# A cross-entropy kernel whose first load is split into two halves of 64 partitions, issued by two engines, with a new table of load widths

## The chip, the cores and the metric

The kernel runs on 1 core of one Trainium2 chip. Time is device time in microseconds of that core; smaller is better. Timed runs of one kernel lie within 0.6 us of each other, most within 0.3. The experiments ran on four chips, each beside the kernel before, whose medians there were 85.26 to 85.42. A profiled execution has a span (first to last instruction), which is 1.8 us shorter than the same execution's time.

## The reference

```python
batch, num_classes = 256, 32000          # logits float32, labels integers
log_probs = logits - np.max(logits, axis=-1, keepdims=True)
log_probs = log_probs - np.log(np.sum(np.exp(log_probs), axis=-1, keepdims=True))
return np.array([-log_probs[i, labels[i]] for i in range(batch)])
```

The kernel leaves the maximum out. Each of the 128 partitions holds two rows one after the other, 64000 columns in all. It takes exp over them with running sums, gathers the logit of each label, and writes ln(sum x exp(-logit)).

## The kernel before

```python
CHUNKS = [
    14848, 12288, 8832, 6528, 4992, 3776, 2752,
    2368, 1856, 1344, 1344, 1152, 1024, 896,
]
...
    def load(i):
        t, base = tiles[i]
        a, b = starts[i], starts[i] + CHUNKS[i]
        nc.sync.dma_start(out=t[:, a - base:b - base], in_=flat[:, a:b])
...
        for i in range(HEAD):          # HEAD = 5: the first five loads, issued at once
            load(i)
        nc.scalar.dma_start(out=lbl[:, :], in_=...)   # labels, on ScalarE's queue
        ...                                           # index arithmetic and two gathers on GpSimd
        exps(0)
        ...                                           # exps(1), then the loads 5 to 13
        nc.scalar.activation(out=eg[:, :], in_=g[:, :], func=AF.Exp, scale=-1.0)
        for i in range(2, len(CHUNKS) - 1):
            exps(i)
```

`exps(i)` is one ScalarE exp over load `i` (two where a load crosses from one row to the next), with the sum as accumulator. A hook moves SyncE's first load ahead of the opening barrier.

The softmax here doesn't subtract the row's maximum and nothing guards it: scores larger than these inputs give would overflow.

## Time and profile before

| | before |
|---|---|
| time, median | 85.26 us (85.17 to 85.44) |
| time and span of the profiled run | 85.8 us, 84.0 us |
| first load lands (first exp starts) | 20.70 us |
| second load lands | 35.91 us |
| last exp starts, ends | 79.98, 80.93 us |

The table is read from the bottom up. The end follows the last exp; ScalarE works nearly without a gap from the landing of the second load (its waits on later loads add up to 0.4 us); the DMA queue is busy all the time up to the last load (92.2% of the span). The prediction below shows the lines.

### The profile page before, as it was taken

The numbers are of one execution on the slowest core, as the hardware profiler recorded it, in microseconds if no ns is written. First come the engines' busy times: TensorE is split into PE (matmuls) and PEld (weight loads), VectorE is DVE, ScalarE is ACT, GpSimd is POOL, SyncE is SP. The second block draws the span as 40 slices with busy tenths as digits, with TensorE's granted clock in tenths as the row PEclk, the third lists the DMA queues.
The fourth block names the chain that finished last, engine by engine and source line by source line (L and its number), as shares of the span: only waits on it lengthen the run. The fifth ranks groups of instructions, "written<-read, shape, count | busy, mean of one in ns | idle before, by whom it ended". The sixth has DMA issues, their size and how long they took to land.

```text
span 84.0 us, 126 instructions
## 1 busy us (share of the span) xinstructions
PE 1.8 (2%) x6; PEld 0.3 (0%) x6; DVE 0.8 (1%) x4; ACT 58.9 (70%) x34; POOL 3.0 (4%) x10
## 2 busy tenths in 40 slices
PE   0000000000000000000000002000000000000050
PEld 0000000000000000000000000000000000000000
DVE  0000000000000000000000200000000000000000
ACT  6000000001999998089999999999999999999960
POOL 3000000000072000000000000000000000000000
DMA  9787899998999989979989999999999999999300
GB/s 424 311 368 339 368 453 453 453 453 375 515 491 421 398 374 421 454 320 521 454 370 407 448 448 403 443 428 417 396 422 418 425 412 420 414 413 405 149 0 0
DMA packets 2226, 32.77 MB, mean 390 GB/s; under 512 B 433, under 2 KB 434, under 8 KB 1202
## 3 DMA queue, kind: packets, MB, share of 16 engines
q1 hardware_dynamic: 2018, 32.77, 92.2%
q10 hardware_dynamic: 144, 0.00, 0.1%
q0 software_dynamic: 64, 0.00, 0.1%
HBM read 32.77 MB, written 0.00 MB: 390 GB/s over the span
## 4 chain that ended last, share of the span: by engine, by line
DMA 74%; issue 13%; ACT 6%; SPq 2%; PE 1%
DMA x<-in_logits_dram 42%; DMA x_tail<-in_logits_dram 33%; ACT x_tail L112 6%; SPq L100 2%; PE lane L160 1%; ACT res L120 0%; ACT x L112 0%; ACT eg L148 0%
## 5 line engine op out<-in xcount | busy, mean ns | idle before, releaser
L112 ACT ACTIVATE x<-x 128x14848 f32<-128x14848 f32 (+5 forms) x6 | 40.7, 6790 | 21.2 <-DMA x<-in_logits_dram 21.2
L112 ACT ACTIVATE x_tail<-x_tail 128x1344 f32<-128x1344 f32 (+6 forms) x8 | 12.2, 1525 | 0.4 <-DMA x_tail<-in_logits_dram 0.4
L112 ACT ACTIVATE x_mid<-x_mid 128x3776 f32<-128x3776 f32 x1 | 3.3, 3349 | 0.0
L135 POOL DMA_INDIRECT g<-in_logits_dram,idx x2 | 2.1, 1036 | 0.6 <-issue 0.3
L91 ACT ACT_TABLE_LOAD x1 | 1.3, 1283 | 0.8 <-PEq L179 0.8
L155 PE MATMUL lane<-diag,sums 128*1 128x128 f32 x2 | 0.6, 396 | 51.0 <-DVE sums L154 51.0
L112 ACT ACTIVATION_READ_ACCUMULATOR x_tail<-x_tail 128x1 f32 x8 | 1.5, 186 | 0.0
L158 PE MATMUL lane<-diag,sums 128*1 128x128 f32 x2 | 0.6, 397 | 28.7 <-DVE sums L157 28.7
L112 ACT ACTIVATION_READ_ACCUMULATOR x<-x 128x1 f32 x6 | 1.1, 187 | 0.0
L120 ACT ACTIVATE res<-lane 1x128 f32<-1x128 f32 x2 | 0.5, 264 | 0.7 <-PE lane L160 0.7
L133 POOL TENSOR_TENSOR idx<-idx,lbl 128x2 int32<-128x2 int32 x1 | 0.2, 193 | 21.4 <-DMA lbl<-in_labels_dram 21.4
L150 DVE TENSOR_SCALAR diag<-ident,eg 128x128 f32<-128x128 f32 x2 | 0.5, 285 | 46.7 <-ACT eg L148 46.7
L160 PE MATMUL lane<-diag,s_last 128*1 128x128 f32 x2 | 0.6, 394 | 0.2 <-ACT x_tail L112 0.2
L157 DVE TENSOR_REDUCE sums<-parts 128x1 f32<-128x11 f32 x1 | 0.2, 164 | 29.1 <-ACT x_tail L112 29.1
masks.py:199 POOL TENSOR_SCALAR_AFFINE_SELECT ident<-ident 128x128 f32<-128x128 f32 x1 | 0.3, 292 | 0.1
L155 PEld LDWEIGHTS lane<-diag,sums 128*1 128x1 f32 x2 | 0.1, 80 | 51.0 <-DVE sums L154 51.0
masks.py:197 POOL MEMSET ident<- 128x128 f32 x1 | 0.2, 194 | 0.0
L154 DVE TENSOR_REDUCE sums<-parts 128x1 f32<-128x3 f32 x1 | 0.2, 156 | 3.7 <-ACT x L112 3.7
L148 ACT ACTIVATE eg<-g 128x2 f32<-128x2 f32 x1 | 0.2, 188 | 0.0
L112 ACT ACTIVATION_READ_ACCUMULATOR x_mid<-x_mid 128x1 f32 x1 | 0.2, 186 | 0.0
L158 PEld LDWEIGHTS lane<-diag,sums 128*1 128x1 f32 x2 | 0.1, 80 | 29.2 <-DVE sums L157 29.2
L131 POOL IOTA idx<- 128x2 int32 x1 | 0.1, 120 | 0.5 <-POOLq L179 0.5
(5 smaller groups left out, 0.5 us busy)
## 6 DMA issues: line engine op xcount, KB each, us to landing
x<-in_logits_dram SPq DMA_DIRECT2D x1, 7424.0 KB, 20.7
x<-in_logits_dram SPq DMA_DIRECT2D x1, 6144.0 KB, 35.1
x<-in_logits_dram SPq DMA_DIRECT2D x1, 4416.0 KB, 45.0
x<-in_logits_dram SPq DMA_DIRECT2D x1, 3264.0 KB, 51.8
x<-in_logits_dram SPq DMA_DIRECT2D x1, 2496.0 KB, 57.2
x_mid<-in_logits_dram SPq DMA_DIRECT2D x1, 1888.0 KB, 17.9
x_tail<-in_logits_dram SPq DMA_DIRECT2D x1, 1376.0 KB
x_tail<-in_logits_dram SPq DMA_DIRECT2D x2, 672.0 KB, 26.8
```

The costliest lines, as they stand in the source:

```text
L91: nc.scalar.preload_act_table_set("natural_log_exp_and_others")
L100: nc.sync.dma_start(out=t[:, a - base:b - base], in_=flat[:, a:b])
L112: nc.scalar.activation(out=t[:, a - base:b - base], in_=t[:, a - base:b - base], func=AF.Exp, accum_out=acc,)
L120: nc.scalar.activation(out=res[0:1, r:ROWS * P:ROWS], in_=lane[r][:, :], func=AF.Ln)
L133: nc.gpsimd.tensor_add(out=idx[:, :], in0=idx[:, :], in1=lbl[:, 0:2 * ROWS:2])
L135: nc.gpsimd.indirect_dma_start(out=g[:, r:r + 1], out_offset=None, in_=logits[:, :], in_offset=bass.IndirectOffsetOnAxis(ap=idx[:, r:r + 1 ...
L148: nc.scalar.activation(out=eg[:, :], in_=g[:, :], func=AF.Exp, scale=-1.0)
L150: nc.vector.tensor_scalar_mul(diag[r][:, :], ident[:, :], eg[:, r:r + 1])
L154: nc.vector.reduce_sum(out=sums[:, 0:1], in_=parts[0][:, :], axis=mybir.AxisListType.X)
L155: nc.tensor.matmul(lane[0][:, :], sums[:, 0:1], diag[0][:, :], start=True, stop=True)
L158: nc.tensor.matmul(lane[1][:, :], sums[:, 1:2], diag[1][:, :], start=True, stop=False)
L160: nc.tensor.matmul(lane[1][:, :], s_last[:, :], diag[1][:, :], start=False, stop=True)
```

## The change

The intent, as I read it, is an earlier start. SyncE and ScalarE each issue half of the first load ahead of the barrier, and a new table makes the first loads wider and the last one narrower, with one load fewer.

```diff
 CHUNKS = [
-    14848, 12288, 8832, 6528, 4992, 3776, 2752,
-    2368, 1856, 1344, 1344, 1152, 1024, 896,
+    15552, 13376, 8960, 7168, 5056, 3584,
+    2816, 2176, 1536, 1280, 1024, 768, 704,
 ]
...
-    first = next(i for i in rest if i.engine == mybir.EngineType.SP and i.opcode == "DMACopy")
...
+    for engine in (mybir.EngineType.SP, mybir.EngineType.Activation):
+        first = next(i for i in rest if i.engine == engine and i.opcode == "DMACopy")
...
-        nc.sync.dma_start(out=t[:, a - base:b - base], in_=flat[:, a:b])
+        if i == 0:
+            nc.sync.dma_start(out=t[:H, a - base:b - base], in_=flat[:H, a:b])
+            nc.scalar.dma_start(out=t[H:, a - base:b - base], in_=flat[H:, a:b])
+        else:
+            nc.sync.dma_start(out=t[:, a - base:b - base], in_=flat[:, a:b])
...
-            if seen[0] == n_of[0] and i == HEAD - 1:
+            if i == turn:
                 ...                    # sum and matmul of the first row
+            if i == turn + 1:
                 log_row(0)
```

`H` is 64. The rest of the diff renames pools and writes the same slots as a list.

More of the change, by code (lines that the diff above doesn't have):

```diff
@@ L10 @@
 P = 128
+H = P // 2
 ROWS = 2
@@ L16 @@
 CHUNKS = [
-    14848, 12288, 8832, 6528, 4992, 3776, 2752,
-    2368, 1856, 1344, 1344, 1152, 1024, 896,
-]
-HEAD = 5
+    15552, 13376, 8960, 7168, 5056, 3584,
+    2816, 2176, 1536, 1280, 1024, 768, 704,
+]
+SLOTS = [0, 1, 2, 3, 4, 1]
+TAIL = len(SLOTS)
+TAIL_SLOT = 0
 def begin_first_load_before_barrier(nc):
@@ L27, in begin_first_load_before_barrier @@
     rest = list(body.instructions)
-    first = next(i for i in rest if i.engine == mybir.EngineType.SP and i.opcode == "DMACopy")
-    rest.remove(first)
     head = list(main.instructions)
-    at = next(
-        k for k, i in enumerate(head) if i.engine == mybir.EngineType.SP and i.opcode == "Drain"
-    )
-    head.insert(at, first)
+    for engine in (mybir.EngineType.SP, mybir.EngineType.Activation):
+        first = next(i for i in rest if i.engine == engine and i.opcode == "DMACopy")
+        rest.remove(first)
+        at = next(k for k, i in enumerate(head) if i.engine == engine and i.opcode == "Drain")
+        head.insert(at, first)
     main.instructions = head
@@ L63 @@
         at += n
-    head = ctx.enter_context(tc.tile_pool(name="head", bufs=1))
+    last = len(CHUNKS) - 1
+    turn = next(i for i in range(len(CHUNKS)) if starts[i] + CHUNKS[i] >= C)
+    big = ctx.enter_context(tc.tile_pool(name="big", bufs=1))
     small = ctx.enter_context(tc.tile_pool(name="small", bufs=1))
+    psum = ctx.enter_context(tc.tile_pool(name="psum", bufs=1, space=bass.MemoryType.PSUM))
+    width = {}
+    for i, s in enumerate(SLOTS):
+        width[s] = max(width.get(s, 0), CHUNKS[i])
     tiles = []
-    for i in range(HEAD):
-        tiles.append((head.tile([P, CHUNKS[i]], F32, name=f"x{i}", tag=f"slot{i}"), starts[i]))
-    mid = head.tile([P, CHUNKS[1]], F32, name="x_mid", tag="slot1")
-    tail = head.tile([P, CHUNKS[0]], F32, name="x_tail", tag="slot0")
-    tiles.append((mid, starts[HEAD]))
-    for i in range(HEAD + 1, len(CHUNKS)):
-        tiles.append((tail, starts[HEAD + 1]))
+    for i, s in enumerate(SLOTS):
+        tiles.append((big.tile([P, width[s]], F32, name=f"x{i}", tag=f"slot{s}"), starts[i]))
+    tail = big.tile([P, width[TAIL_SLOT]], F32, name="x_tail", tag=f"slot{TAIL_SLOT}")
+    assert sum(CHUNKS[TAIL:]) <= width[TAIL_SLOT]
+    tiles += [(tail, starts[TAIL])] * (len(CHUNKS) - TAIL)
     n_of = [sum(1 for ps in pieces[:-1] for q in ps if q[2] == r) for r in range(ROWS)]
@@ L83 @@
     diag = [small.tile([P, P], F32, name=f"diag{r}") for r in range(ROWS)]
-    psum = ctx.enter_context(tc.tile_pool(name="psum", bufs=1, space=bass.MemoryType.PSUM))
     lane = [psum.tile([1, P], F32, name=f"lane{r}") for r in range(ROWS)]
@@ L106, in exps @@
         for a, b, r in pieces[i]:
-            if i == len(CHUNKS) - 1:
+            if i == last:
                 acc = s_last[:, :]
@@ L124 @@
     with tc.manual_schedule():
-        for i in range(HEAD):
+        first = len(set(SLOTS))
+        for i in range(first):
             load(i)
@@ L140 @@
             )
-        exps(0)
-        for i in range(HEAD + 1, len(CHUNKS)):
-            if i == HEAD + 1:
-                exps(1)
-                load(HEAD)
+        done = 0
+        for i in range(first, len(CHUNKS)):
+            slot = SLOTS[i] if i < TAIL else TAIL_SLOT
+            while done <= SLOTS[:first].index(slot):
+                exps(done)
+                done += 1
             load(i)
@@ L150 @@
             nc.vector.tensor_scalar_mul(diag[r][:, :], ident[:, :], eg[:, r:r + 1])
-        for i in range(2, len(CHUNKS) - 1):
+        for i in range(done, last):
             exps(i)
-            if seen[0] == n_of[0] and i == HEAD - 1:
+            if i == turn:
                 nc.vector.reduce_sum(out=sums[:, 0:1], in_=parts[0][:, :], axis=mybir.AxisListType.X)
                 nc.tensor.matmul(lane[0][:, :], sums[:, 0:1], diag[0][:, :], start=True, stop=True)
+            if i == turn + 1:
                 log_row(0)
@@ L158 @@
         nc.tensor.matmul(lane[1][:, :], sums[:, 1:2], diag[1][:, :], start=True, stop=False)
-        exps(len(CHUNKS) - 1)
+        exps(last)
         nc.tensor.matmul(lane[1][:, :], s_last[:, :], diag[1][:, :], start=False, stop=True)
```

## The prediction

Passages on rules and causes that no trace or run of this case shows are cut out of the recorded text, and the cuts are marked. The sum comes to 80.7 + 4.2 = 84.9 us. The three parts of g are estimates from what the trace shows: an issue of 0.40 us, engines that start up to 0.9 us late, 0.7 us more in the first round. The first rival is a first load at half rate; its 218 GB/s is half of the 435 GB/s of the second load. Its premise, all engines in one half at a time, was a supposition; the packet records of the kernel after show it for about three quarters of the first load. From here on this rival is called the collision. Three things that the text says of the hardware can be seen in the packet records of before. From 6.1 to 18.1 us, 16 label packets of 16 bytes start with each round of 16 packets of 59392 bytes, and the last 32 start at 19.3 to 20.7. The first two loads landed at 20.70 and 35.91, 0.3 and 0.6 us after the end of their last packets (20.36, 35.28). A 59392-byte packet took 2.4 to 3.1 us in the first round and, from the third on, nearly always the 2.19 that the text computes.

> **What bounds the kernel now.** I read the page first (engine shares, DMA row, chain), then the time-ordered instructions of ScalarE and of the DMA issues, then stretches of DMA rate. ScalarE is busy 70% of the span and the DMA queue 92%. The whole kernel is one stream of 32.77 MB of logits in 14 loads, with one exp over each load behind it.
>
> ```profile
> ACT  6000000001999998089999999999999999999960
> DMA  9787899998999989979989999999999999999300
> ...
> q1 hardware_dynamic: 2018, 32.77, 92.2%
> ...
> DMA 74%; issue 13%; ACT 6%; SPq 2%; PE 1%
> ```
>
> The ScalarE row has two holes, before the first load (slices 1 to 9) and before the second (slice 16). After those it is full to the end, and so is the DMA row until slice 37. From the second load on, transfer and exp run neck and neck.
>
> The instructions in time order show where each hands over to the other (start, duration, then idle and releaser in brackets):
>
> ```profile
> 20.70 12.58 ACT L112 ACTIVATE x<-x 128x14848 f32<-128x14848 f32 x1 [18.60 <-DMA x<-in_logits_dram]
> ...
> 35.94 10.44 ACT L112 ACTIVATE x<-x 128x12288 f32<-128x12288 f32 x1 [2.57 <-DMA x<-in_logits_dram]
> 46.28 0.19 ACT L112 ACTIVATION_READ_ACCUMULATOR x<-x 128x1 f32 x1
> 46.38 0.19 ACT L148 ACTIVATE eg<-g 128x2 f32<-128x2 f32 x1
> ...
> 76.20 1.32 ACT L112 ACTIVATE x_tail<-x_tail 128x1344 f32<-128x1344 f32 x1 [0.18 <-DMA x_tail<-in_logits_dram]
> ...
> 79.98 0.95 ACT L112 ACTIVATE x_tail<-x_tail 128x896 f32<-128x896 f32 x1
> ...
> 81.69 0.27 ACT L120 ACTIVATE res<-lane 1x128 f32<-1x128 f32 x1 [0.67 <-PE lane L160]
> ```
>
> The first exp starts at 20.70 but the second load lands only at 35.91 (chain of waits), so ScalarE idles 2.57 us after the first exp: the arrival of the first load alone is not critical. Two things are: the landing of the second load (35.91), from which ScalarE has 45.1 us to its last exp's end, and the landing of the last load. That one I read from the issues: it is issued at 64.44 and needs 15.5 us, so 79.9, which is when the last exp starts (79.98). So the end is bound by the DMA stream by a hair, with ScalarE almost as late. After the last exp come two matmuls, the logarithm and the store: 85.26 - 81.03 = 4.23 us from the end of the last exp and its accumulator to the timed end, which the change does not touch.
>
> **Rates.** ScalarE: the 14848-wide exp took 12576 ns and the 896-wide one 949 ns, so 0.833 ns per column and 202 ns fixed; successive exps start one duration apart, since the accumulator read overlaps. Check: this rule, run from 35.94 through all remaining exps with the few waits on landings put in, ends at 81.0, against 81.03 seen. DMA: from 35.91 to 79.9, 36864 columns in 12 loads took 44.0 us, 1.195 ns per column. About 1.18 of this is the wide-load rate (512 bytes per column at the 435 GB/s below) and the rest some 0.05 us per load.
>
> ```profile
> 1.00:1.40 0.40, 0.00 (x0) 0.00 (x0) 0.00 (x0) 0.40 (x1) 0.33 (x3) 1.00 5.44 1782
> 1.40:2.30 0.90, 0.00 (x0) 0.00 (x0) 0.00 (x0) 0.69 (x1) 0.15 (x1) 1.00 0.74 264
> 2.30:3.70 1.40, 0.00 (x0) 0.00 (x0) 0.00 (x0) 0.00 (x0) 0.00 (x0) 1.00 0.00 0
> 3.70:4.50 0.80, 0.00 (x0) 0.00 (x0) 0.00 (x0) 0.00 (x0) 0.00 (x0) 1.00 2.43 1039
> ...
> 21.00:36.00 15.00, 0.00 (x0) 0.00 (x0) 0.00 (x0) 12.43 (x3) 2.27 (x3) 1.00 1.01 435
> ```
>
> These are stretches; the last column is GB/s, with a packet's bytes counted where it starts. One packet is one row of a load (59392 bytes): 1782 GB/s for 0.4 us is 12 packets, 264 for 0.9 us is 4. So 12 of the 16 DMA engines begin between 1.0 and 1.4 us, four up to 0.9 us later, and the second round of packets starts only around 4.1, 2.9 us after the first. At 435 GB/s over 16 engines (27.2 each) a packet should take 2.19 us. The beginning therefore costs 1.0 us to the first packet, some 0.7 us in a long first round, and up to 0.9 us on the late engines; a load lands with its last engine.
>
> [...] the 2 KB label load, on ScalarE's ring, took 22.0 us to land, since its tiny packets alternated with 59 KB ones. [...] the first issue here took 0.40 us, so little is to be had. [...] No transfer of half the partitions is in this trace[...].
>
> **The change, part by part.**
> 1. Wider first two loads: 28928 columns instead of 27136. 1792 x 1.18 ns = 2.1 us later landing of the second load: 38.0 with nothing gained.
> 2. Two half issues, one more ahead of the barrier, each for half the rows. I estimate a gain g = 0.8 us at the second load's landing: 0.15 for shorter issues, 0.5 of the 0.9 us by which late engines trail, 0.15 of the 0.7 us of the long first round. This is the softest figure; nothing to 1.5 is possible. Second load: 37.2.
> 3. ScalarE's work from there: 13376 + 35072 = 48448 columns x 0.833 = 40.4 us, 13 exps (the third load spans both rows) x 0.21 = 2.75, the small exp of the gathered logits 0.1, the first logarithm 0.2: 43.45 us. Last exp ends at 37.2 + 43.45 = 80.7.
> 4. DMA from there: 35072 x 1.195 = 41.9, so the last load lands at 79.1; its exp, 704 wide instead of 896, takes 0.79 + 0.1 for the accumulator: 80.0. It is 0.7 us ahead of ScalarE, which takes over as the bound of the end.
> 5. One load and one exp fewer: about 0.05 us of DMA, 0.2 us of ScalarE, already counted. Moving the first logarithm one exp earlier moves it, not removes it. Later loads are issued after the second exp, near 48.6, while the first five (50112 columns, 25.7 MB) keep the queue fed to about 62: no starvation.
>
> Sum: 80.7 + 4.2 = 84.9 us, 0.4% faster. With g = 0 it is 85.7, with g = 1.5 it is 84.2. The wider head spends most of what the start saves, and what the smaller last load saves is beneath ScalarE's new bound.
>
> **Rivals.**
> [...] If the 16 engines march in step through partitions 0 to 63, then 64 to 127, the first load runs at half rate: 7.96 MB at 218 GB/s is 36.6 us, not 18.3. The time would be 102 to 104. For it: [...] 12 engines starting within 0.4 us. Against: both rings hold packets from the start, so the two halves can be in flight together [...]; and the new table makes the first load wider, which no one would choose after seeing it slow. I give it a tenth.
> *A late label.* The label load now stands behind a half load in ScalarE's ring, and its eight packets per engine alternate with the second load's, so it lands near the second load (37 to 38) instead of 22.8. Before, the gathers landed about 13 us after it at 1.8 us rounds; now the rounds are of the 8960-wide load (1.3 us), so I estimate 10 us: 47 to 48. The exp that reads them stands behind the second exp, which ends at 37.2 + 11.35 = 48.6. In the trace before it had over 10 us to spare; now about 1. If it is late by 1 or 2 us, ScalarE waits, and as ScalarE is the bound the whole of it shows: 86 to 87.
> *A larger gain at the start.* If all three costs of the start went, g would be near 2 and the time 83.7, still not 2%.
> *DMA remains the bound.* If the tail streams slower than 1.195 ns per column the last landing decides; 0.7 us of slack hides that, so the time would stay near 85.
>
> **Range and chances.** The sum without mishap spans 84.2 to 85.7; a moderate gather wait stretches it up to 87, a bigger start gain down to 83.7. Two percent is 1.7 us: faster needs g above 2.1, slower needs the collision or a long gather wait. So 0.08, 0.79, 0.13.
>
> **What would show it.** Right: second exp starting at 37 to 37.5 with 2 to 3 us idle before it; no releasing DMA in front of the last exps, only back-to-back ScalarE; label landing near 37; the exp of gathered logits without a wait; last load landed some 0.7 us before its exp. Wrong: a first exp after 25 us (collision); a wait on the gathered logits in front of that small exp (late label); the last exps waiting on DMA (step 4); a second exp at 38 or later (no gain at the start).

## More of the kernel before

For the experiments I also need the DMA rate in mid-stream, during the third load. This is a view of stretches of the kernel before; the last column is GB/s (the one before it is the DMA engines' busy share):

```profile
34.00:39.00 5.00, 0.00 (x0) 0.00 (x0) 0.00 (x0) 3.06 (x1) 0.00 (x0) 1.00 0.95 410
39.00:44.00 5.00, 0.00 (x0) 0.00 (x0) 0.00 (x0) 5.00 (x1) 0.00 (x0) 1.00 1.05 452
```

The rate is 410 and 452 GB/s with the engines fully busy, the pace of an undisturbed stream here (435 GB/s during the second load).

## The result, and the profile after

The time after is 103.91 us (103.8 to 104.1), before 85.26. The ratio is 1.2186, 95% interval 1.2158 to 1.2215: 22% slower. I had written 84.9, with a range up to 87.

The page of the kernel after, busy tenths and rate in 40 slices of 2.55 us, then the queues with packets, MB and share of 16 engines' span:

```profile
ACT  4000000000000002999990999999999999999981
DMA  9091959919090918987995999999899999999910
GB/s 390 0 390 24 366 122 268 366 24 390 0 390 0 390 42 294 650 357 336 441 566 239 436 450 450 405 393 495 371 412 468 399 416 424 410 423 401 405 46 0
...
q1 hardware_dynamic: 1810, 28.79, 75.9%
q10 hardware_dynamic: 224, 3.98, 18.4%
```

For 15 slices the rate jumps between about 390 and nearly nothing. A packet's bytes and time are counted where it starts, so this is a picture of starts: all 16 engines begin a packet at about the same time, then none does for nearly two slices. Queue 10 is ScalarE's. Its half load is 64 packets of 62208 bytes (of the other 160 packets, 128 have 16 bytes, the labels, and 32 have 4). 18.4% of 102.0 us on 16 engines is 300 engine-us, or 4.69 us per packet: 13.3 GB/s per engine. The packet records agree: 4.66 us, against 2.19 us for the 59392-byte packets before. They also show the order. All 16 engines take a packet of SyncE's half at 1.3 to 2.2 us, all take one of ScalarE's at 5.5 to 6.7, all go back to SyncE's at 10.2 to 11.4, and so on to 39 us.

The instructions in time order (start, duration, idle and releaser in brackets):

```profile
0.00 0.55 SPq L110 DMA_DIRECT2D x<-in_logits_dram  x1
0.12 0.53 ACTq L111 DMA_DIRECT2D x<-in_logits_dram  x1
...
1.48 1.28 ACT L100 ACT_TABLE_LOAD   x1 [1.48 <-PEq L196]
...
40.25 13.16 ACT L125 ACTIVATE x<-x 128x15552 f32<-128x15552 f32 x1 [37.49 <-DMA x<-in_logits_dram]
...
55.88 11.35 ACT L125 ACTIVATE x<-x 128x13376 f32<-128x13376 f32 x1 [2.37 <-DMA x<-in_logits_dram]
56.10 0.19 POOL L147 TENSOR_TENSOR idx<-idx,lbl 128x2 int32<-128x2 int32 x1 [53.88 <-DMA lbl<-in_labels_dram]
...
98.17 0.77 ACT L125 ACTIVATE x_tail<-x_tail 128x704 f32<-128x704 f32 x1
```

The first load lands at 40.2 instead of 20.7, the second at 55.85 instead of 35.91, 19.9 us later. From there to the end of the last exp it is 43.06 us against 44.99 before, 1.9 us less. 19.9 less 1.9 is 18.0, the difference of the two profiled runs (103.83 and 85.8). So the loss lies wholly before the second load's landing. Eight packets per engine at 4.66 instead of 2.30 us (what 62208 bytes need at the pace before) make 18.9 us, and the wider loads 2.1. The remaining -1.1 I put down to the start: the first packets are no slower than the later ones (before, 2.9 us in the median of the first round instead of 2.19), and the engines end the second load within 0.4 us of their median instead of 1.2. As a remainder this is not shown; the profiled run of before was itself 0.5 us slower than the median.

Theory: what counts is which partitions a load writes. One that lies wholly in partitions 0 to 63, or wholly in 64 to 127, moves at about half rate (211 GB/s over most of this first load); one with partitions of both halves doesn't (435 GB/s for the whole second load of before). I call this the **partition theory**. I also supposed that it takes all engines in the same half at the same time; experiment 10 was to test that. Why it should be so, no trace here shows. Rivals: two queues alternating halve an engine's rate (**two rings**; a ring is the queue of packets that one issuing engine feeds); loads of 64 partitions are slow of themselves (**size**); only loads at the very start are (**start**); the new table is at fault (**table**).

### The profile page after: what moved, and what is told of

The parts are those of the page before. It is cut to its first block, busy times and chain, and to the rows that moved or that the text cites. A ratio compares the mean times of both kernels' runs of the same rounds, so it can differ in the third digit from the quotient of the medians.

```text
span 102.0 us, 126 instructions
## 1 busy us (share of the span) xinstructions
PE 1.7 (2%) x6; PEld 0.3 (0%) x6; DVE 0.8 (1%) x4; ACT 58.0 (57%) x32; POOL 3.0 (3%) x10
## 3 DMA queue, kind: packets, MB, share of 16 engines
q10 hardware_dynamic: 224, 3.98, 18.4%
## 4 chain that ended last, share of the span: by engine, by line
ACT 54%; DMA 39%; another core or an unknown queue 2%; PE 1%; issue 1%; DVE 0%; ACTq 0%
ACT x L125 45%; DMA x<-in_logits_dram 39%; ACT x_tail L125 9%; PE lane L177 1%; PE lane L175 1%; ACT res L133 0%; DVE sums L174 0%; ACT eg L164 0%; ACTq L125 0%
## 5 line engine op out<-in xcount | busy, mean ns | idle before, releaser
L125 ACT ACTIVATE x<-x 128x15552 f32<-128x15552 f32 (+6 forms) x7 | 46.1, 6585 | 39.9 <-DMA x<-in_logits_dram 39.9
L125 ACT ACTIVATE x_tail<-x_tail 128x2816 f32<-128x2816 f32 (+6 forms) x7 | 9.9, 1412 | 0.0
```

The source lines that it names most:

```text
L125: nc.scalar.activation(out=t[:, a - base:b - base], in_=t[:, a - base:b - base], func=AF.Exp, accum_out=acc,)
```

## The experiments

Eleven kernels, all with correct outputs. Experiments 1 to 4 start from the kernel after, 5 to 11 from the kernel before.

### 1. e1_taper_alone: the table without the halves

```diff
-            nc.sync.dma_start(out=t[:H, a - base:b - base], in_=flat[:H, a:b])
-            nc.scalar.dma_start(out=t[H:, a - base:b - base], in_=flat[H:, a:b])
+            nc.sync.dma_start(out=t[:, a - base:b - base], in_=flat[:, a:b])
```

(The hook moves SyncE's load alone.)

> The new table of loads with one whole first load of 128 partitions, issued by SyncE ahead of the barrier as before. Both theories of the slow start [...] make the loss vanish: first packets take 2.3 us each, first load landing near 21.5, second near 38. From the arithmetic of my prediction with no gain at the start: last exp ends 81.4, time 85.7 (0.5% slower than before), ScalarE and not DMA bounding the tail. If the table itself carries part of the loss, the time is above 87.

Measured: 85.42 us (85.32 to 85.89), ratio 1.0022 (1.0008 to 1.0036). In time order:

```profile
21.76 13.16 ACT L124 ACTIVATE x<-x 128x15552 f32<-128x15552 f32 x1 [19.67 <-DMA x<-in_logits_dram]
...
37.91 11.35 ACT L124 ACTIVATE x<-x 128x13376 f32<-128x13376 f32 x1 [2.89 <-DMA x<-in_logits_dram]
```

The landings came as computed (21.7 and 37.9), and the time is 0.3 us below the 85.7 that I had computed. The table costs at most 0.4% and is not the cause.

### 2. e2_column_halves: two issuers, two rings, all partitions

```diff
-            nc.sync.dma_start(out=t[:H, a - base:b - base], in_=flat[:H, a:b])
-            nc.scalar.dma_start(out=t[H:, a - base:b - base], in_=flat[H:, a:b])
+            m = (a + b) // 2
+            nc.sync.dma_start(out=t[:, a - base:m - base], in_=flat[:, a:m])
+            nc.scalar.dma_start(out=t[:, m - base:b - base], in_=flat[:, m:b])
```

> The first load in halves again, by SyncE and ScalarE ahead of the barrier, but halves of the columns, each of all 128 partitions. Two rings alternate on each engine as in the changed kernel. [...] 31104 bytes take 1.15 us, the first load lands near 21.5, time 85 to 86. Two-ring theory (alternating rings halve an engine's rate): 2.3 us per 31104-byte packet, first load landing near 40, time near 104. It also shows whether the label load, behind ScalarE's half, lets the gathered logits come too late: I expect labels near 37, gathers near 47, no wait.

Measured: 85.21 us (85.13 to 85.28), ratio 0.9988 (0.9974 to 1.0001). Its page has for ScalarE's queue:

```profile
q10 hardware_dynamic: 288, 3.98, 11.2%
```

128 of these are the half load's packets, of 31104 bytes. 11.2% of 83.5 us on 16 engines, by 128, is 1.17 us, 26.6 GB/s per engine: full pace, with two rings alternating. Two rings are ruled out. The stretches of this run's first load:

```profile
1.00:11.00 10.00, 0.00 (x0) 0.00 (x0) 0.00 (x0) 1.19 (x1) 0.56 (x3) 1.00 1.02 407
11.00:21.00 10.00, 0.00 (x0) 0.00 (x0) 0.00 (x0) 0.00 (x0) 0.00 (x0) 1.00 1.09 469
```

The kernel after, over most of its first load:

```profile
11.00:39.00 28.00, 0.00 (x0) 0.00 (x0) 0.00 (x0) 0.00 (x0) 0.00 (x0) 1.00 0.95 211
```

The same bytes by the same two issuers: over 400 GB/s in halves of columns, 211 in halves of partitions.

This run also tests the late label at a normal pace. The labels landed at 37.4 and the gathers at 48.1. The exp that reads them started at 48.63 right behind the second exp and did not wait, with 0.5 us to spare.

### 3. e3_one_ring: both partition halves from SyncE

```diff
-            nc.scalar.dma_start(out=t[H:, a - base:b - base], in_=flat[H:, a:b])
+            nc.sync.dma_start(out=t[H:, a - base:b - base], in_=flat[H:, a:b])
```

(The hook moves both ahead of the barrier.)

> Partition halves 0 to 63 and 64 to 127 both issued by SyncE, one after the other, so one ring and no alternation. [...] 4.66 us per packet, first load near 40, time near 104. Two-ring theory: 2.3 us per packet, time near 85.7.

Measured: 105.3 us, one look. Most packets took 4.85 us (one round of the eight 4.61) and the second half landed at 41.45. The page shows the same picture of starts:

```profile
GB/s 385 0 385 0 385 24 361 144 241 313 72 385 0 385 0 331 331 558 434 331 352 532 443 429 429 382 399 421 465 383 445 405 421 425 413 407 412 403 34 0
```

With no alternation between halves it is as slow, so the halves are the cause and not the second ring. Why 4.85 and not 4.66 is open.

### 4. e4_middle_half: 64 partitions, 32 from each half

```diff
-            nc.sync.dma_start(out=t[:H, a - base:b - base], in_=flat[:H, a:b])
-            nc.scalar.dma_start(out=t[H:, a - base:b - base], in_=flat[H:, a:b])
+            nc.sync.dma_start(out=t[32:96, a - base:b - base], in_=flat[32:96, a:b])
+            nc.scalar.dma_start(out=t[:32, a - base:b - base], in_=flat[:32, a:b])
+            nc.scalar.dma_start(out=t[96:, a - base:b - base], in_=flat[96:, a:b])
```

(The hook moves all three ahead of the barrier.)

> SyncE takes partitions 32 to 95 [...], ScalarE takes 0 to 31 and 96 to 127 in two loads. [...] SyncE's four packets per engine take 2.3 us each, ScalarE's four 4.66 us each [...], 27.9 us in all, first load near 30, time about 94. A theory that a load of 64 partitions is slow for its size or its rows in HBM: SyncE's packets take 4.66 too, first load near 40, time near 104.

(SyncE's load has partitions of both halves, each of ScalarE's two loads has partitions of one half alone. 2.3 us is the time that 62208 bytes need at the pace before, 4.66 us what they took in the kernel after.)

Measured: 96.92 us, one look; first load complete at 33.2. The direction is that of the partition theory, the size is 3 us off. ScalarE's packets took 4.6 to 5.0 us (expected 4.66). SyncE's four rounds took 3.1, 2.9, 2.3 and 2.9 us (expected 2.3 each). The round of 2.3 us is the only one that follows another of SyncE's; the slower ones start while some engines are still in a packet of ScalarE's. My expectation had left out this overlap. Experiment 11 repeats the test without it.

### 5. e5_halves_alone: the halves on the old table

```diff
+        if i == 0:
+            nc.sync.dma_start(out=t[:64, a - base:b - base], in_=flat[:64, a:b])
+            nc.scalar.dma_start(out=t[64:, a - base:b - base], in_=flat[64:, a:b])
+        else:
```

(The hook is that of the kernel after.)

> The table of loads of before, with only the first load in partition halves by SyncE and ScalarE ahead of the barrier. If the collision explains all of the loss, each 59392-byte packet takes 4.45 us instead of 2.19, the second load lands near 53 and the time is 102 to 103, the new table adding about 1 to 2 us of its own only through its wider first load. If the table and the halves worsen each other, the time is under 98.

Measured: 103.06 us, one look; packets 4.39 us; second load at 52.6. The halves alone cost 17.8 of the 18.65 us. With the 0.1 to 0.2 us of the table alone (experiment 1) that makes about 18, so the two parts worsen each other by some 0.7 us only; that the wider first load now runs at half rate fits this in direction.

### 6 and 7. e6_column_halves_old_table and e7_column_halves_one_issuer: is there anything to gain at the start?

```diff
+        if i == 0:
+            m = (a + b) // 2
+            nc.sync.dma_start(out=t[:, a - base:m - base], in_=flat[:, a:m])
+            nc.scalar.dma_start(out=t[:, m - base:b - base], in_=flat[:, m:b])   # e7: nc.sync
+        else:
```

(The hook moves both ahead of the barrier.)

> The table of before, first load in column halves of all 128 partitions by SyncE and ScalarE ahead of the barrier. With the new table the column halves brought the second load 0.6 us forward (37.9 to 37.3). If the end is bound by the DMA stream as the trace of before showed, the whole 0.6 us comes through here: 84.6 to 84.8, 0.6 to 0.8% faster than before. If ScalarE bounds it anyway, or the late label load costs, it stays at 85.2.

> As the run before in this list, but both column halves are issued by SyncE. If the gain comes from two engines issuing at once, it is gone: 85.3. If it comes from smaller first packets (a short first round, so that late engines trail less), it stays: 84.6 to 84.8.

Measured: 85.56 us (85.47 to 85.69), ratio 1.0032 (1.0017 to 1.0047), and 85.34 us (85.2 to 85.74), ratio 1.001 (0.9989 to 1.0032). Both expectations of a gain missed. In their profiled runs the second load did land earlier than in that of before (35.2 and 35.0 against 35.9), yet the time did not follow. One reason can be seen: the profiled execution of before was a slow one of its kind (85.8 us, median 85.26), so its landings are not typical. So was that of experiment 1 (85.89, median 85.42), from which I had the 0.6 us. The rest can be located in the traces: from the second load's landing to the last one's the stream took 44.4 and 44.25 us, against 44.0 before, and from the last exp's end to the end of the span it took 3.3 us against 3.1. Why is open. In experiment 6 the exp of the gathered logits also waited 0.18 us for them (in experiment 5 it was 0.17), though not on the chain that ended last. On the old table a split of the first load, by two issuers or one, is worth nothing that shows. On the new one it is worth a little: experiment 2 is 0.2 us below experiment 1 in the median, and the ranges of their runs (85.13 to 85.28 and 85.32 to 85.89) do not touch.

### 8. e8_third_load_halves: the halves in mid-stream

```diff
+        if i == 2:
+            nc.sync.dma_start(out=t[:64, a - base:b - base], in_=flat[:64, a:b])
+            nc.sync.dma_start(out=t[64:, a - base:b - base], in_=flat[64:, a:b])
+        else:
```

> Kernel of before with its third load (8832 columns) in partition halves, both by SyncE, far from the barrier and in mid-stream; the first load whole. [...] the collision has nothing to do with the start or the barrier: 35328-byte packets take 2.6 to 2.75 us instead of 1.31, 10.5 to 11.5 us more in the stream, time 95.5 to 97. A theory that the start of the kernel (cold DMA engines, barrier) made the halves slow: 85.3.

Measured: 97.68 us, one look. The same stretches as shown for before:

```profile
34.00:39.00 5.00, 0.00 (x0) 0.00 (x0) 0.00 (x0) 2.42 (x1) 0.00 (x0) 1.00 1.00 212
39.00:44.00 5.00, 0.00 (x0) 0.00 (x0) 0.00 (x0) 5.00 (x1) 0.00 (x0) 1.00 1.00 205
```

Half the rate at the same busy share: the engines look busy and move half. From the second round on, nearly all packets took 2.55 to 2.77 us instead of 1.31. The loss is 0.7 us above the range I gave. The start theory falls.

### 9 and 10. e9_pieces and e10_pieces_lag: shifting the engines against each other

```diff
+        if i == 0:
+            n = CHUNKS[1]                                                        # e10 only
+            nc.sync.dma_start(out=tiles[1][0][64:96:4, :], in_=flat[64:96:4, :n]) # e10 only
+            for c in range(0, b, b // 4):
+                d = c + b // 4
+                nc.sync.dma_start(out=t[:64, c:d], in_=flat[:64, c:d])
+                nc.sync.dma_start(out=t[64:, c:d], in_=flat[64:, c:d])
+        else:
```

> Control for the next run. The table of before; the first load cut into four column pieces, each piece into partition halves 0 to 63 and 64 to 127, all eight issued in turn by SyncE (the first ahead of the barrier). [...] 14848-byte packets take 1.1 to 1.2 us instead of 0.55, first load landing near 39 to 41, time 102 to 106.

> The same with one extra load ahead of them, of 8 partitions (64, 68, to 92; 12288 columns, overwritten later by the second load), which should occupy 8 of the 16 engines for about 1.8 us, nearly one piece's 2.2 us. [...] packets return to 0.55 to 0.7 us, the first load lands near 22 to 25 and the time is 86 to 89. If loads of 64 partitions are slow of themselves, nothing changes: 102 to 106. [...]

(In experiment 10 the figures after the first cut, up to 86 to 89 us, are for the case that the slow rate needs all engines in the same half at the same time. That was a supposition of mine.)

Measured: 102.95 and 107.54 us, one look each. In experiment 9 the 14848-byte packets took 1.0 to 1.2 us after the first two rounds, about as expected, and the first load landed at 38.4, just before the range. In experiment 10 nothing improved, and the time lies 1.5 us above all that I had listed:

```profile
GB/s 149 186 202 213 230 197 208 225 197 236 202 213 225 202 321 229 446 335 558 316 450 441 428 454 379 418 454 400 403 448 423 415 417 422 414 413 409 261 7 0
```

The extra load, in partitions 64 to 92, held eight engines from 1.5 to about 4.2 us. The remaining eight began their first packets, in partitions 0 to 63, at 3.3 to 3.5 us, and these already took 0.8 to 1.1 us while the first eight were still elsewhere. That could mean that the engines that slow each other are among the eight themselves. But an engine's first packet is long without any collision too (2.4 to 3.1 us instead of 2.19 in the kernel before), so it isn't shown. The lag was also short, some 0.7 us. This run tells nothing for or against lockstep (all engines in the same half at the same time); whether engines slow each other in a load of 64 partitions, and which, stays open.

### 11. e11_third_load_middle: the clean form of experiment 4

```diff
-            nc.sync.dma_start(out=t[:64, a - base:b - base], in_=flat[:64, a:b])
-            nc.sync.dma_start(out=t[64:, a - base:b - base], in_=flat[64:, a:b])
+            for p, q in ((32, 96), (0, 32), (96, 128)):
+                nc.sync.dma_start(out=t[p:q, a - base:b - base], in_=flat[p:q, a:b])
```

(Against experiment 8.)

> Third load of the table of before again, all by SyncE in mid-stream, but as partitions 32 to 95, then 0 to 31, then 96 to 127. [...] the 64 partitions from 32 to 95 [...] their four packets per engine take 1.31 us each as in the whole load; the two loads of 32 partitions [...] their four packets take 2.62 to 2.76 us. In all some 5.5 us more than before, half of what the halves cost: time 90.5 to 92.5. If loads of 64 partitions are slow for their size: all eight packets 2.6 to 2.8 us, time 97 to 98.

(Partitions 32 to 95 are of both halves, the two groups of 32 of one half each. 1.31 us is what these packets took in the whole load of before, 2.62 twice that.)

Measured: 92.58 us, one look, 0.1 us above the range. The stretches:

```profile
34.00:39.00 5.00, 0.00 (x0) 0.00 (x0) 0.00 (x0) 3.36 (x1) 0.00 (x0) 1.00 0.93 396
39.00:44.00 5.00, 0.00 (x0) 0.00 (x0) 0.00 (x0) 5.00 (x1) 0.00 (x0) 1.00 1.05 226
```

While partitions 32 to 95 load, the rate is 396 GB/s, as with the whole load. When the two groups of 32 follow, it is 226. Packet by packet: three rounds of 16 took 1.31 to 1.33 us each, the fourth as well except three packets that overlap the next load; the four rounds after it took 2.2 to 2.8. Same number of partitions, same row size, same queue as in experiment 8, and only the choice of partitions differs. The size theory falls and the partition theory stands, as the account that fits every run: halves 0 to 63 and 64 to 127 at 205 to 212 GB/s (experiment 8), 32 to 95 at 396. It says which loads are slow; what in the hardware makes them slow was not shown. One rival is left untested: each partition always takes its own stretch of the logits in HBM, so no run tells which partitions are written together from which addresses are read together. (The addresses by themselves aren't slow: those of partitions 32 to 63 ran at half rate in experiment 8 and at full rate here.)

## Why the prediction was wrong

**What bounds the kernel** was right. The second load's landing governs the rest, and the whole loss came in through it. The sign that I had named for the collision, a first exp after 25 us, came: 40.25.

**Step 2, the two half issues, is the step that failed.** It put down a gain of 0.8 us at the second load's landing (37.2); it landed at 55.85. The collision stood among the rivals with 102 to 104 us, and the time was 103.91. I gave it a tenth on two arguments, and both were bad. The first was that "both rings hold packets from the start, so the two halves can be in flight together". The packet records show otherwise: 16 packets are open at a time, the rings come in turn, and for about three quarters of the first load all open packets belong to the same half. The label load that I read in the trace of before had already shown packets taking turns; I used it for the labels and not for the load. The second was that the new table makes the first load wider "which no one would choose after seeing it slow". That is a guess about how a change came about and says nothing of the machine. Beyond them the tenth was my estimate: no trace at hand held a transfer of half the partitions.

**The 0.8 us of gain at the start** was too large even without the collision. On the new table the early halves of columns gained 0.2 us (experiment 2 against 1); on the old one (experiments 6 and 7) nothing. Of its three terms, the 0.15 us for shorter issues failed outright: the first issue, of 64 rows, took 0.55 us (0.53 on ScalarE), one of 128 rows 0.40 (0.37 on ScalarE in experiment 2).

**Step 1** held: the wider loads brought the second landing to 37.9 in experiment 1, where I computed 38.0.

**Step 3** was close: 43.04 us in experiment 1 from the second exp's start to the last one's end, where I had 43.45.

**Step 4** held in direction. The last load of the kernel after was issued at 81.18 and needed 16.9 us, so it landed at 98.1, and its exp started at 98.17. DMA is ahead by 0.1 us (0.3 in experiment 1), not by 0.7. Two terms made the difference: from the second landing on the stream took 42.2 us (42.0 in experiment 1) where I had 41.9, and ScalarE took 0.4 us less than I had, as step 3 shows.

**The 4.23 us after the last exp** was mis-sized as well. It took the end from a median of 85.26 and the exp from a profiled run of 85.8. Within one run it is 4.8 us. By luck the errors of step 3 (0.4 us too long) and of this term (0.6 too short) largely cancel: with no gain at the start the sum gave 85.7, and experiment 1 measured 85.42 (85.89 in its profiled run).

**The late label** went as estimated in experiment 2 (labels 37.4, gathers 48.1, no wait). In the kernel after, everything moved back together and it did not wait either. With the old table, whose second exp is shorter, a wait did come, of 0.2 us (experiments 5 and 6).

No version clearly beats the kernel before. Experiment 2 comes nearest, at 0.9988, and its interval reaches 1.0001.

## What to carry to other kernels

If a transfer must be split, split it by columns, not by partitions 0 to 63 and 64 to 127: in this kernel the halves of partitions ran at 211 GB/s, the halves of columns at over 400. A busy share near 1 does not mean full rate (1.00 at 205 GB/s in experiment 8, 1.05 at 452 before); compare the packet's time with its size. Keep guesses about why someone made a change out of the odds.
